# One ring of five PSUM banks for scores and products of maxima, and the product of maxima last in its slot

## The chip, the core and the metric

The kernel runs on one core of a Trainium2 chip. The metric is the device time of one execution in microseconds. Before the change the median of three runs is 2717.88 us (2717.04 to 2718.28). One execution was profiled: 2720.0 us, with 2718.2 us from the first to the last instruction.

Engines are named as in the profile: PE is TensorE's matmuls, PEld its loads of the stationary operand, DVE is VectorE, ACT is ScalarE, POOL is GpSimd, SP is the queue that issues DMAs.

## The reference, cut to what matters

One transformer layer on 2048 rows of width 1024, in float32, followed by a norm. It has a retention branch in two directions, an attention branch and a feed-forward block. What the change touches is the attention:

```python
def _dense_attention(q, k, v):
    s = jnp.einsum('bqkgd,bskd->bkgqs', q, k).astype(jnp.float32) * ATT_SCALE
    p = jax.nn.softmax(s, axis=-1).astype(v.dtype)
    return jnp.einsum('bkgqs,bskd->bqkgd', p, v)
```

There are 8 query heads of width 64 on 2 key heads, and 2304 keys (2048 of the sequence and 256 of the context). A softmax needs the largest score of each row, or a number near it, to be subtracted ahead of the exponential.

## The kernel before, in words

Work on attention is cut into 32 groups: one tile of 128 query rows by one of the two key heads, with its 4 query heads side by side (512 columns). A group goes through two passes over the 2304 keys, 18 steps each.

- First pass, for the row maxima. Step i is `piece` (L164): a product of queries and keys, rows on the partitions and 512 keys across, into a PSUM bank (one matmul, L169, or two half ones, L173). `maximum` (L175) reduces it on DVE to one negated maximum a row (L182). After 18 steps `least` (L184) joins them, `turn` (L190) transposes the result into a PSUM bank with four matmuls (L193), and `rows` (ACT, L196) and `rows2` (DVE, L200) write it as a high and a low part into rows of the query tile `qr`, so that the score matmul adds it.
- Second pass. `scores` (L202) makes the scores turned, 128 keys on the partitions and 512 query columns across: a first matmul (L206) and a second (L207) that holds the subtracted maxima and so needs `qr` from `rows2`. `exp` (L209, ACT) reads the bank, `cast` (ACT, L216) makes a float16 high part of two steps at once, `low` the low part (on POOL, L224, or DVE, L226), and `values` (L228) multiplies both by the values, 24 small matmuls (L240 to L242) for two steps. `combine` (DVE, L247, L252) divides by the sum.

The order on every engine is written out by hand. Time is counted in slots. `on(k, phase, fn)` puts a step into slot k, and a loop over the slots runs the phases of each slot in the order of PHASES. So within each engine the instructions stand in the order slot, phase, and within a phase in the order in which they were registered. An engine never passes a waiting instruction of its own. With 18 slots to a group (NK) and LAG = 22, group n has its piece i in slot 18n + i, the maximum of it one slot later, `least` in slot 18n + 18, `turn` and `rows` in slot 18n + 20, `rows2` in slot 18n + 21, score i in slot 18n + 22 + i, its exponential one slot later, and values j in slot 18n + 22 + 2j + 8, which is always an even slot. So in most slots PE has the score of one group and the piece of the next, and in every second slot values.

Group 0 has its pieces in the stage before, and the last 22 slots have no pieces.

Beside attention the slots carry other work ("pe" is its phase on PE), with a period of 35 slots per tile of rows:

- retention (from slot 66 + 35n): one score step (8 matmuls, L1370), two slots of state products (L1349), four slots of `head` (L1379 to L1381); `mask` and `update` on DVE.
- the output projection, `output_tile`, with k = 109 + 35n: the transposes of retention and attention results at k - 11 and k - 6 (L1475) with `part` behind them (ACT L1480, DVE L1482); output products (three matmuls each, L1490 to L1492) at k plus the 16 PLACES 0 to 3, 5 to 8, 11 to 14 and 16 to 19, the first eight for one half of the columns and the rest for the other half in the same bank, with `add` (DVE, L1497) behind each half in the phase "early" of slots k + 10 and k + 20; then `square` (ACT, L1502) in the phase "cast" of slot k + 20, `norm` (ACT, L1516) in the phase "late" of slots k + 24 and k + 25, its transposes `turn_x` (L1521) in slots k + 25 and k + 27, and `modulate` (DVE, L1526) in the phase "early" one slot behind each.

PSUM has eight banks. In this stage two hold the side work (`bank(0)`, `bank(1)`), one the output of `values`, and five belong to the pool psS: three under the tag "mp", which pieces and the turned tile take in turn, and two under the tag "st", which scores take in turn. A tile that takes a bank waits for the last reader of the tile that had it: a score waits for the exponential of the score two slots earlier, a piece for the maximum of the piece three places earlier.

Of the kernel before, what the change touches and what calls it, by code (L numbers as in the profile page):

```python
# [11 lines left out]
F32 = mybir.dt.float32  # L12
# [10 lines left out]
P = 128  # L23
# [32 lines left out]
def layer_kernel(ctx: ExitStack, tc: tile.TileContext, a: dict, out: bass.AP):  # L56
# [87 lines left out]
    class Group:  # L144
# [43 lines left out]
                nc.vector.tensor_reduce(mt[:, :, c], nm, axis=AX.X, op=ALU.min)  # L188

        def turn(self):  # L190
            self.m = psS.tile([P, 4, P], F32, name="mp", tag="mp", bufs=3)
            for h in range(4):
                nc.tensor.transpose(self.m[:, h], self.mt[:, h], ident)  # L193

# [5 lines left out]
            nc.vector.scalar_tensor_tensor(lo, self.m[96:], 1 / ROW, lo, op0=ALU.mult, op1=ALU.subtract)  # L200

        def scores(self, kt):  # L202
            ps = self.s[kt] = psS.tile([P, 512], F32, name="st", tag="st")
            k = slice(kt * P, (kt + 1) * P)
            q = self.qr.rearrange("p x h t -> p x (h t)")
            mm(ps, ks[:, self.g, k], q[:, 0], start=True, stop=False)  # L206
            mm(ps, ks2[:, self.g, k], q[:, 1], start=False, stop=True)  # L207
# [50 lines left out]
    with ExitStack() as st:  # L258
# [154 lines left out]
        def turned(fn):  # L413
            def turn(x):
                x["ps"] = columns(x["b"][:64], 4)

            def use(x, q):
                at(q, "turn", turn, x)
                at(q + 1, "work", lambda: fn(x["ps"][:, :, :, 0]))

            return use
# [337 lines left out]
        def value_parts(q0):  # L759
# [39 lines left out]
            for i in range(3):  # L799
                at(q0 + 3 + i, "extra", greatest, i)  # L800
                at(q0 + 11 + i, "extra", parts, i)
            at(q0 + 7, "turn", turn)
            at(q0 + 8, "work", scale)

# [25 lines left out]
        def ff_scales(q0):  # L830
# [71 lines left out]
            at(q0, "dma", load)  # L902
            at(q0 + 1, "extra", greatest)
            at(q0 + 3, "turn", turn)
            at(q0 + 4, "work", whole)
            at(q0 + 6, "extra", scales)
# [306 lines left out]
    def pool(stack, name, bufs=1, **kw):  # L1213
        return stack.enter_context(tc.tile_pool(name=name, bufs=bufs, reuse_waits="tile", **kw))
# [4 lines left out]
    psS = pool(attn, "psS", 2, space=PSUM)  # L1219
# [29 lines left out]
    def on(k, phase, fn, *args):  # L1249
        events.setdefault((k, phase), []).append((fn, args))  # L1250

    def run(k, phase):
        for fn, args in events.pop((k, phase), ()):
            fn(*args)


    chain, settled = [], set()
# [21 lines left out]
    def attention():  # L1279
        for n, g in enumerate(groups):  # L1280
            k = NK * n
            if n > 0:
                on(k - 14 if n >= EARLY else k + NK - 6, "dma", g.load)
            else:
                on(k + 2, "dma", g.load)
            if n >= EARLY:
                on(k - 1, "late", g.minima, sm)
                for i in range(NK):
                    on(k + i, "piece", g.piece, i, psS, "mp", 3)
                    on(k + i + 1, "maximum", g.maximum, i)  # L1290
            on(k + NK, "chain", g.least, mts[n % 2])
            on(k + NK + 2, "scores", g.turn)
            on(k + NK + 2, "cast", g.rows)
            on(k + NK + 3, "early", g.rows2)
            k += LAG
            for i in range(NK):
                on(k + i, "scores", g.scores, i)
                on(k + i + 1, "exp", g.exp, i)
            for j in range(NK // 2):
                on(k + 2 * j + 3, "cast", g.cast, j)  # L1300
                if j in POOL_PAIRS:
                    on(k + 2 * j + 4, "low", g.low, j)
                else:
                    for i in range(2):
                        on(k + 2 * j + 4 + i, "low", g.low, j, i)
                on(k + 2 * j + 8, "values", g.values, j)
            k += NK + 7
            on(k, "early", g.combine, ats)
        return NK * len(groups) + LAG + 10
# [301 lines left out]
    for i in range(3):  # L1611
        on(19 + 2 * i, "begin", more_keys, 0, i)
        on(26 + 4 * i, "late", more_keys, 1, i)
    done = attention()
    retention(25)
    output_weights(44)
# [333 lines left out]
    def prelude(k0):  # L1950


        on(k0 - 8, "dma", fetch_w1, 0)
        on(k0 - 2, "late", sum_w1, 0, *SUMS1[0])
        on(k0 - 1, "late", sum_w1, 0, *SUMS1[1])
        on(k0, "begin", open_early)
        for n in range(7):
            on(k0 + (n // 2 if n < 4 else 12 + 2 * n), "dma", fetch_h, 0, n)
            on(k0 + 2 + 2 * n, "late", form_w1, 0, n)
            on(k0 + 3 + 2 * n, "late", lower_w1, 0, n)  # L1960
        on(k0, "late", sum_w1, 0, *SUMS1[2])
        on(k0 + 3, "late", sum_w1, 0, *SUMS1[3])
        on(k0 + 16, "dma", fetch_w1, 1)
        on(k0 - 12, "dma", fetch_gate)
        for i in range(4):
            for k in range(4):
                on(k0 + 14 + 4 * i + k, "pe", up_part, 0, i, k)
            on(k0 + 17 + 4 * i, "late", up_out, 0, i)
            on(k0 + 24 + 2 * i, "late", sum_w1, 1, *SUMS1[i])
# [10 lines left out]
        early_job(b, pairs0 + 60 + 80 * b)  # L1980
    on(made_at + 1, "begin", open_late)
    prelude(done)
    PHASES = ("begin", "scores", "piece", "maximum", "early", "exp", "cast", "low", "chain", "pe", "values")
    PHASES += ("late", "dma")
    with tc.manual_schedule():
        for k in range(min(events)[0], max(events)[0] + 1):
            for phase in PHASES:
                run(k, phase)
# [5 lines left out]
        for b in range(2 * NB):  # L1994
            g = 7 * b
# [51 lines left out]
        g = NU * NS  # L2047
# [15 lines left out]
        for lo, g0 in ((0, g + 10), (4, g + 14)):  # L2063
# [3 lines left out]
            for m in range(lo, lo + 4):  # L2067
                k = g0 + 1 + m % 4 // 2
# [3 lines left out]
        g = NU * (2 * NS - 1)  # L2072
# [125 lines left out]
```

## Time and profile before

| what | value |
|---|---|
| median of three runs | 2717.88 us (2717.04 to 2718.28) |
| the profiled execution | 2720.0 us, span 2718.2 us |
| granted TensorE clock, mean | 0.991 |
| PE busy over the span | 2627.0 us (97%) |
| DVE, ACT, POOL busy over the span | 2101.8, 1585.8, 1416.2 us |
| first and last start of a score matmul (L206) | 626.5 and 1496.5 us |
| PE's wait at L206 for ACT's exponential | 13.5 us in 22 waits |

How to read it: a line of the timeline is start, duration, engine, line, operation, output and inputs, count, and in brackets the idle time of the engine before it with what ended that. The ends of matmuls are modelled, and they overlap: a matmul of 512 columns has 0.38 us in the rows, and the next one can start 0.21 or 0.22 us after it. Idle time counts from the modelled end, and short gaps aren't shown. A row of the table of waits is the waiting instruction, what released it, the total in us, the number of waits and the longest.

### The profile page before, as it was taken

The page shows a single profiled execution, that of the slowest core. Times are in us where ns is not written, and L with a number is a line of the kernel's source. Part 1 is how long each engine was busy: PE and PEld are TensorE (multiplying, and loading weights), DVE is VectorE, ACT ScalarE, POOL GpSimd, SP SyncE. Part 2 cuts the span into 40 slices and gives each one's busy share as a digit, 9 for nine tenths or more (in the row PEclk, how much of TensorE's full clock was granted, in tenths as well). Part 3 has the DMA queues.
Part 4 walks back from the last instruction along what each step waited for, and adds up shares of the span by engine and source line. Part 5 has one row for each costly group of instructions (what it writes and reads, how often), then busy time and mean ns, then how long its engine had stood idle before and what let it go on. Part 6 is the DMA issues. An engine that isn't in the chain of part 4 may idle for free.

```text
span 2718.2 us, 49296 instructions
## 1 busy us (share of the span) xinstructions
PE 2627.0 (97%) x19015; PEld 1418.7 (52%) x19015; DVE 2101.8 (77%) x3323; ACT 1585.8 (58%) x2656; POOL 1416.2 (52%) x1262
## 2 busy tenths in 40 slices
PE   6999999998999999999999899999999999999997
PEld 2545754555666666666666444444444444444443
DVE  4857578878977888888887477898899856666676
ACT  3733763327877778887778475555554554344332
POOL 2623673475656667787777444455557621111155
PEclk8999999999999999999999999999999999999999
DMA  7478858674112223333322655565657332222223
GB/s 253 148 235 293 246 170 274 199 264 150 57 51 68 72 74 93 130 90 122 100 77 80 223 190 175 193 205 188 193 178 269 115 117 86 78 86 86 78 85 132
DMA packets 274197, 402.31 MB, mean 148 GB/s; under 512 B 107237, under 2 KB 162405, under 8 KB 271658
## 3 DMA queue, kind: packets, MB, share of 16 engines
q1 hardware_dynamic: 270938, 394.44, 44.6%
q10 hardware_dynamic: 3024, 4.72, 0.5%
q8 instruction: 149, 2.44, 0.4%
q14 instruction: 86, 0.70, 0.1%
HBM read 294.08 MB, written 105.00 MB: 147 GB/s over the span
## 4 chain that ended last, share of the span: by engine, by line
PE 48%; DVE 4%; ACT 2%; issue 1%; DMA 1%; POOL 0%; SPq 0%; POOLq 0%; ACTq 0%; DVEq 0%
PE pu L1698 7%; PE pu L1700 7%; PE pu L1699 7%; PE pd L1877 6%; PE pd L1875 6%; PE pd L1876 6%; PE st L206 1%; PE st L207 1%; PE mp L169 1%; PE bank L1492 1%; PE bank L1490 1%; PE bank L1491 1%; PE o L240 1%; PE o L242 1%; PE o L241 1%
## 5 line engine op out<-in xcount | busy, mean ns | idle before, releaser
L224 POOL TENSOR_TENSOR plo<-p,phi 128x512 f16<-128x512 f32 x320 | 393.4, 1250 | 165.7 <-ACT phi L216 118.0
L182 DVE TENSOR_REDUCE nm<-mp 128x1 f32<-128x512 f32 (+1 forms) x576 | 386.4, 684 | 118.3 <-PE mp L169 91.6
L212 ACT ACTIVATE p<-st 128x512 f32<-128x512 f32 x576 | 339.6, 600 | 136.5 <-PE st L207 126.5
L1698 PE MATMUL pu<-hf,w1f 128*128 128x512 f16 x896 | 340.6, 380 | 4.8 <-ACT w L1715 4.8
L1700 PE MATMUL pu<-hf,w1f 128*128 128x512 f16 x896 | 340.6, 380 | 0.0
L1699 PE MATMUL pu<-hf,w1f 128*128 128x512 f16 x896 | 340.5, 380 | 0.0
L216 ACT ACTIVATE phi<-p 128x1024 f16<-128x1024 f32 x288 | 304.6, 1058 | 0.0
L642 PE MATMUL pso<-wlo,h 128*128 128x512 f16 (+1 forms) x816 | 295.7, 362 | 2.2 <-DVE wlo L539 2.2
L641 PE MATMUL pso<-whi,h 128*128 128x512 f16 (+1 forms) x816 | 296.0, 363 | 1.3 <-ACT whi L538 1.3
L643 PE MATMUL pso<-whi,h 128*128 128x512 f16 (+1 forms) x816 | 295.7, 362 | 0.0
L226 DVE TENSOR_TENSOR plo<-p,phi 128x512 f16<-128x512 f32 x256 | 231.5, 905 | 12.8 <-ACT phi L216 9.0
L240 PE MATMUL o<-wv,plo 128*128 128x65 f16 x2304 | 237.9, 194 | 1.6 <-DVE ma L252 1.3
L241 PE MATMUL o<-wv,phi 128*128 128x64 f16 x2304 | 237.8, 192 | 0.0
L242 PE MATMUL o<-wv,phi 128*128 128x65 f16 x2304 | 236.8, 193 | 0.0
L206 PE MATMUL st<-qr,ks 128*128 128x512 f16 x576 | 218.7, 380 | 14.1 <-ACT p L212 13.5
L240 PEld LDWEIGHTS <-plo 128*128 128x128 f16 x2304 | 211.3, 97 | 29.3 <-issue 4.7
L1901 DVE SCALAR_TENSOR_TENSOR acc<-pd,scv,acc 128x512 f32<-128x512 f32 x248 | 183.2, 743 | 53.0 <-PE pd L1877 50.3
L241 PEld LDWEIGHTS <-phi 128*128 128x128 f16 x2304 | 210.2, 98 | 25.3
L207 PE MATMUL st<-qr,ks 128*128 128x512 f16 x576 | 217.9, 378 | 3.8 <-DVE qr L200 3.2
L1663 POOL TENSOR_TENSOR w1s<-w1r 128x512 f32<-128x512 f32 x64 | 92.0, 1437 | 231.7 <-ACT w L1737 160.3
L242 PEld LDWEIGHTS <-phi 128*128 128x128 f16 x2304 | 210.5, 97 | 0.0
L169 PE MATMUL mp<-ks,qr 128*128 128x512 f16 x512 | 194.3, 380 | 8.4 <-DMA qr<-aq 5.7
(382 smaller groups left out, 6377.6 us busy)
## 6 DMA issues: line engine op xcount, KB each, us to landing
w2t<-w2f SPq DMA_DIRECT2D x98, 512.0 KB, 4.3
wm<-in_w_ff SPq DMA_DIRECT2D x64, 512.0 KB, 5.5
w1r<-in_w_ff SPq DMA_DIRECT2D x64, 512.0 KB, 4.6
w2f<-w2f SPq DMA_DIRECT2D x98, 256.0 KB, 2.4
wmr<-in_w_mod SPq DMA_DIRECT2D x32, 512.0 KB, 5.0
w2r<-in_w_ff SPq DMA_DIRECT2D x32, 512.0 KB, 4.7
hf<-hp SPq DMA_DIRECT2D x56, 256.0 KB, 3.1
hf<-hf SPq DMA_DIRECT2D x14, 1024.0 KB, 7.2
```

Source lines behind the costliest of these rows:

```text
L182: nc.vector.tensor_reduce(dst, src, axis=AX.X, op=ALU.max, negate=True)
L212: nc.scalar.activation(self.p[kt // 2][:, kt % 2], self.s.pop(kt), AF.Exp, scale=HD**-0.5)
L216: nc.scalar.activation(hi, self.p[j], AF.Copy)
L224: nc.gpsimd.tensor_tensor(lo[:, i], p[:, i], hi[:, i], op=ALU.subtract)
L240: mm(o, lo[:, i, c], v[:, : HD + 1], start=first, stop=False, **more)
L241: mm(o[:, :HD], hi[:, i, c], v[:, VL : VL + HD], start=False, stop=False, **more)
L242: mm(o, hi[:, i, c], v[:, : HD + 1], start=False, stop=last, **more)
L641: mm(self.ps[:, c], hi[:, k], wh, start=k == 0, stop=False)
L642: mm(self.ps[:, c], hi[:, k], wl, start=False, stop=False)
L1698: mm(pu[c], whi, hi, start=first and k == 0, stop=False, **more)
L1699: mm(pu[c], whi, lo, start=False, stop=False, **more)
L1700: mm(pu[c], wlo, hi, start=False, stop=k == 3, **more)
```

## The change

Pieces, the turned tile and scores share one tag, "sp", with five banks, in place of three and two. And the phase "piece" stands behind "values", at the end of PE's work of a slot, in place of right behind "scores". What is computed doesn't change.

```diff
         def turn(self):
-            self.m = psS.tile([P, 4, P], F32, name="mp", tag="mp", bufs=3)
+            self.m = psS.tile([P, 4, P], F32, name="mp", tag="sp", bufs=5)
...
         def scores(self, kt):
-            ps = self.s[kt] = psS.tile([P, 512], F32, name="st", tag="st")
+            ps = self.s[kt] = psS.tile([P, 512], F32, name="st", tag="sp", bufs=5)
...
                 for i in range(NK):
-                    on(k + i, "piece", g.piece, i, psS, "mp", 3)
+                    on(k + i, "piece", g.piece, i, psS, "sp", 5)
                     on(k + i + 1, "maximum", g.maximum, i)
...
-    PHASES = ("begin", "scores", "piece", "maximum", "early", "exp", "cast", "low", "chain", "pe", "values")
+    PHASES = ("begin", "scores", "maximum", "early", "exp", "cast", "low", "chain", "pe", "values", "piece")
     PHASES += ("late", "dma")
```

In PE's order a slot is now score, turned tile where there is one, side work, values, piece. With one score and one piece a slot, the tile five places back is, for a score, the piece of three slots earlier, and for a piece, the score of two slots earlier; so a score waits for DVE's maximum and a piece for ACT's exponential. For two slots behind each turned tile the places are shifted by one.

## The prediction

> **What bounds the kernel now.** I read the page first, then the time by stage, the table of waits of the attention stage, and the timelines of three places in it.
>
> ```profile
> PE 2627.0 (97%) x19015; PEld 1418.7 (52%) x19015; DVE 2101.8 (77%) x3323; ACT 1585.8 (58%) x2656; POOL 1416.2 (52%) x1262
> ```
>
> ```profile
> 626.00:700.00 74.00, 68.57 (x883) 45.43 (x882) 70.95 (x122) 65.54 (x100) 48.52 (x41) 0.99 0.40 130
> 1200.00:1300.00 100.00, 94.35 (x1138) 63.40 (x1137) 88.55 (x150) 78.84 (x122) 78.65 (x68) 1.00 0.37 119
> 626.00:1440.00 814.00, 787.28 (x9545) 523.86 (x9544) 692.10 (x1204) 652.82 (x1014) 575.00 (x509) 1.00 0.29 88
> ```
>
> The columns are the stretch, its length, then PE, PEld, DVE, ACT and POOL busy. The stage that holds both tiles is TensorE's: 787.28 us busy of 814, at the full granted clock (1.00). So at most 27 us of visible gaps are there to be won. VectorE follows at 692.10, with 70.95 of 74 in the opening.
>
> ```profile
> L206 PE MATMUL st<-qr,ks x576: 376/379/631, 626.5 to 1496.5; 128*128 128x512 f16 x192
> ```
>
> ```profile
> DVE nm L182 <- PE mp L169: 87.2, 120, 3.1
> PE st L206 <- ACT p L212: 13.5, 22, 1.5
> ACT junk L1502 <- DVE xr L1497: 9.1, 9, 2.1
> PE st L207 <- DVE qr L200: 3.2, 6, 0.9
> PE mp L169 <- DVE nm L182: 2.6, 2, 2.3
> PE o L240 <- DVE ma L252: 1.3, 2, 0.9
> ```
>
> (us in total, times, longest.) 576 slots start between 626.5 and 1496.5: 1.51 us a slot. The one large wait of TensorE is the one the ring is about: a score bank whose exponential isn't done, 13.5 us in 22 waits. VectorE, on the other hand, waits 87.2 us for the products: its maximum mostly starts when the product is ready, so it follows wherever the product goes.
>
> **The change, part by part.** No instruction is added or removed, no DMA is moved; only TensorE's order and the owners of five banks change. The product is passed by the slot's side products ("pe") and by its values; VectorE's and ScalarE's own orders stay.
>
> *What the ring takes away.* A score now waits for the maximum of three slots ago, and a product for the exponential of two slots ago, about a slot's content later than the score did. The two waits of one tile period:
>
> ```profile
> 768.15 0.38 PE L206 MATMUL st<-qr,ks 128*128 128x512 f16 x1
> 768.36 0.38 PE L207 MATMUL st<-qr,ks 128*128 128x512 f16 x1
> 770.25 0.38 PE L206 MATMUL st<-qr,ks 128*128 128x512 f16 x1 [0.57 <-ACT p L212]
> 774.22 0.66 PE L1521 MATMUL bank<-ident,xn 128*128 128x128 f32 x4
> ```
>
> ```profile
> 768.57 1.06 ACT L1502 ACTIVATE junk<-xr 128x1024 bf16<-128x1024 f32 x1 [0.30 <-DVE xr L1497]
> 769.63 1.06 ACT L212 ACTIVATE p<-st 128x512 f32<-128x512 f32 x2
> 773.43 0.73 ACT L1516 ACTIVATE xn<-xr,cy_f 128x512 f32<-128x512 f32 x1
> ```
>
> A matmul lasts 0.38 but the next starts 0.21 later (768.15, 768.36), so a wait costs its idle plus 0.17: 0.74 at 770.25, and 13.5 + 22 x 0.17 = 17 us for all 22. What is late next: ScalarE has no gap behind the square of 768.57, and the transposes at 774.22 start 0.06 behind the xn that it makes in that same run (773.43 + 0.73). If the score stops waiting at 770.25, TensorE waits that much longer at 774.22. Gain: 0. In every other tile (35 slots a tile, values in every second slot) there is room:
>
> ```profile
> 824.51 0.38 PE L206 MATMUL st<-qr,ks 128*128 128x512 f16 x1 [0.89 <-ACT p L212]
> 829.04 0.60 PE L1521 MATMUL bank<-ident,xn 128*128 128x128 f32 x4
> 831.48 0.38 PE L206 MATMUL st<-qr,ks 128*128 128x512 f16 x1 [0.47 <-ACT p L212]
> ```
>
> ```profile
> 827.68 0.74 ACT L1516 ACTIVATE xn<-xr,cy_f 128x512 f32<-128x512 f32 x1
> ```
>
> Here xn ends at 828.42, 0.62 ahead of 829.04: of the 1.06 at 824.51 some 0.57 is won, and behind the transposes the 0.64 at 831.48 too, 1.2 in all. Some 7 tiles of each kind lie in the stage: 7 x 1.2 = 8 us, and I allow 2 more for the waits of the opening and the end. Against it, the square waits for VectorE's sum (9 of its starts); that sum stands behind a maximum, so it comes about 0.6 later by what follows: 9 x 0.6 = 5 us lost where ScalarE sets the pace. What is left is about 5 us; the bounds are -1 and 17.
>
> *What the later product costs: the row maxima.* VectorE does the maximum first in each slot; what stands behind it comes later too. First the rows2 step (L200), which the next group's second score matmul needs:
>
> ```profile
> 765.91 0.38 PE L169 MATMUL mp<-ks,qr 128*128 128x512 f16 x1
> 766.13 0.38 PE L1490 MATMUL bank<-wo,ah 128*128 128x512 f16 x1
> 766.56 0.38 PE L1492 MATMUL bank<-wo,al 128*128 128x512 f16 x1
> 767.50 0.38 PE L206 MATMUL st<-qr,ks 128*128 128x512 f16 x1
> 767.93 0.38 PE L169 MATMUL mp<-ks,qr 128*128 128x512 f16 x1
> ```
>
> ```profile
> 766.33 0.69 DVE L182 TENSOR_REDUCE nm<-mp 128x1 f32<-128x512 f32 x1 [1.04 <-PE mp L169]
> 767.05 0.70 DVE L200 SCALAR_TENSOR_TENSOR qr<-mp,qr 32x512 f16<-32x512 f32 x1
> 767.78 0.75 DVE L1497 SCALAR_TENSOR_TENSOR xr<-bank,sco,xr 128x512 f32<-128x512 f32 x1
> ```
>
> Now: product 765.91, maximum 0.42 later, rows2 0.72 after that, ended 767.75; the matmul that needs it starts 768.36, 0.6 to spare. After: the product goes behind three matmuls and 24 values, to 767.50 - 0.21 = 767.29; maximum 767.71, rows2 768.43 to 769.13. The matmul stays due at 768.36, so TensorE waits 0.8. Between the two lies just one slot: 0.65 where it holds nothing else (767.50 to 768.15), 0.65 more with three output matmuls, which leaves 0.15. By the planner's places 10 of a tile's 35 slots are empty so: of 30 groups 9 x 0.8 + 21 x 0.1 = 9 us. In 6 of them the matmul waits today (3.2 us), VectorE being late; they pay little more: 8 us. Bounds: 3, where VectorE is late in most groups and the product doesn't set it, and 30 x 0.8 = 24.
>
> *The first half's sum (L1497).* The second half's first output product needs its bank:
>
> ```profile
> 1077.25 0.38 PE L169 MATMUL mp<-ks,qr 128*128 128x512 f16 x1
> 1078.19 0.38 PE L206 MATMUL st<-qr,ks 128*128 128x512 f16 x1
> 1079.27 0.38 PE L169 MATMUL mp<-ks,qr 128*128 128x512 f16 x1
> 1079.48 0.38 PE L1490 MATMUL bank<-wo,rh 128*128 128x512 f16 x1
> ```
>
> ```profile
> 1077.67 0.69 DVE L182 TENSOR_REDUCE nm<-mp 128x1 f32<-128x512 f32 x1 [0.60 <-PE mp L169]
> 1078.39 0.75 DVE L1497 SCALAR_TENSOR_TENSOR xr<-bank,sco,xr 128x512 f32<-128x512 f32 x1
> ```
>
> The product of 1077.25 goes to 1077.98, its maximum to 1078.40, the sum to 1079.12, done 1079.87. The output product, now ahead of its slot's own product, is due at 1079.27: 0.65 of waiting. That holds where the slot between has no values, half of 16 tiles: 5 us (bounds 0 and 10).
>
> *Hand-overs of the same form without a row of their own wait:* the retention scores behind the first modulate (L1526), the attention transposes behind the second, the next group's first values behind combine (L252). Each is one or two VectorE steps behind a maximum and due a slot later. From below 0, from above 0.65 as in the last case: 8 tiles x 2 + 31 x 10/35 groups, 25 x 0.65 = 16. I take half, 8, since a part of these slots is shared with ScalarE's stretch.
>
> *The ring's own new wait.* From a product's end to the score that takes its bank lie two slots (3.0 us) where three lay before the next product. VectorE lags in the opening and at 1200 to 1300 (rows above), and has cost 2.6 us in two waits. From -2.6 (the wait just goes) to 12 (one slot, 1.5, in each of eight such stretches): I take 3, near the row there is.
>
> **Sum:** -5 + 8 + 5 + 8 + 3 = +19. The four losses aren't independent: each holds TensorE while VectorE catches up, and one within ScalarE's stretch costs nothing. I count 15 of the 24: +10 us. The profiled execution took 2720.0, so 2730; the median of the runs lies 2.1 under it, so 2728.
>
> **Rivals.** *Faster:* the ring is worth its whole wait, 17 us with 4 given to VectorE: 2705. For it: 13.5 us is the largest wait, and VectorE is idle for 122 of 814 us, so it could catch up. Against it: the rows at 774.22, and two VectorE steps of 0.7 that don't fit in a slot of 0.65. The Trainium skill speaks for it (Perfetto Trace Analysis, Optimization Strategy): the same gap again and again on the engine that should be full can mean too few buffers. The trace agrees on the wait at 824.51, not on the one at 770.25, where ScalarE is full.
> *No change:* ScalarE's waits go (8 to 10 us) and VectorE, where it is late anyway, costs as much: 2718.
> *Slower by far:* every new wait at its price (24), no gain from ScalarE, and the square late in all tiles: 2742. It decides if the sum of L1497 stands behind a waiting maximum in most tiles.
> *The ring doesn't do what it says:* the turned tile takes a place too, so for two slots after it a score waits for the exponential two back, as before. Price: 2 of 18 slots, under 17 x 2/18 = 2 us of the gain; it changes no sign and is in the cases above.
>
> **How the numbers follow.** Forecast 0.50, with 2723 to 2736 as its own range; slower by far 0.14; no change 0.20; faster 0.16. A measurement of this kernel tells about 0.2% (5.4 us) from no change. So slower 0.64, same 0.20, faster 0.16. The range leaves out the faster half of the faster case and the end of the slowest: 2708 to 2742.
>
> **What would show it.** Right: the score's wait for ScalarE falls from 13.5 to under 5; the second score matmul's for qr grows from 3.2 us in 6 to some 10 in 15 or more; the output product's for the sum appears with about 0.5 a time; x transposes wait for xn; the square waits longer than 9.1. Wrong: if the wait for qr stays under 5 us, the costs of the later product are misjudged, and the time is below 2718.

## The result and the profile after

The changed kernel takes 2758.7 us (median of four runs, 2754.45 to 2761.04) against 2718.08 us (median of four as well): a ratio of 1.0143, with a 95% interval of 1.0131 to 1.0155, some 39 us slower. The profiled execution has a span of 2757.0 us, 38.8 us more than before. The score matmuls now run for 908.0 us, where they ran for 870.0:

```profile
L206 PE MATMUL st<-qr,ks x576: 376/379/634, 623.6 to 1531.6; 128*128 128x512 f16 x192
```

So nearly the whole loss, 38.0 of 38.8 us, lies in the attention stage. The stretch from 626 us to the last score by engine, of the kernel before and then of the changed one (length, then busy time of PE, PEld, DVE, ACT, POOL):

```profile
626.00:1496.50 870.50, 841.54 (x10241) 561.16 (x10240) 729.23 (x1271) 699.91 (x1089) 618.16 (x549) 1.00 0.29 88
```

```profile
626.00:1531.60 905.60, 853.35 (x10239) 559.07 (x10238) 745.70 (x1267) 700.10 (x1086) 622.63 (x548) 0.99 0.27 84
```

TensorE's idle time grows from 29.0 to 52.3 us, by 23.3. Its busy time grows as well, by 11.8 us for the same matmuls. Most of that is waiting too: the modelled matmul lasts 0.17 us longer than its place in the pipeline, so the first 0.17 us of each wait count as busy, and waits shorter than that show no gap at all. Counted from the start of one matmul to the start of the next, what goes beyond the usual distance sums to some 43 us before and to 74 to 79 after, by which distance is taken as usual. So 31 to 36 us of waiting stand against the 35 us by which the stretch is longer.

Rows of the table of waits of this stage in the changed kernel, taken from 596 us on, as before the change (waiting instruction, releaser, us in total, times, longest):

```profile
DVE nm L182 <- PE mp L169: 116.1, 157, 2.9
ACT junk L1502 <- DVE xr L1497: 20.9, 14, 2.1
PEld bank L1521 <- ACT xn L1516: 12.3, 13, 1.8
PE st L207 <- DVE qr L200: 10.1, 20, 0.8
PE bank L1521 <- ACT xn L1516: 6.0, 6, 1.3
PE st L206 <- DVE nm L182: 6.0, 9, 1.6
PE bank L1490 <- DVE xr L1497: 5.8, 9, 1.6
PE bank L1475 <- DVE u L1526: 5.8, 9, 2.0
PE o L240 <- DVE ma L252: 5.4, 7, 1.3
PE st L206 <- ACT p L212: 2.3, 3, 1.0
```

The wait that the ring is about has all but gone (13.5 us before, 2.3 now). In its place stand six TensorE waits of 5 to 10 us: four for a VectorE step that stands behind a maximum (qr, xr, u, ma), one for the maximum itself, which now frees the score's bank, and one for ScalarE's xn. VectorE itself waits longer for the product: 116.1 us, 87.2 before. The place whose rows the prediction works out, in the changed kernel, in order of time:

```profile
768.80 0.38 PE L206 MATMUL st<-qr,ks 128*128 128x512 f16 x1
769.00 0.69 DVE L182 TENSOR_REDUCE nm<-mp 128x1 f32<-128x512 f32 x1 [1.36 <-PE mp L169]
769.72 0.70 DVE L200 SCALAR_TENSOR_TENSOR qr<-mp,qr 32x512 f16<-32x512 f32 x1
770.45 0.75 DVE L1497 SCALAR_TENSOR_TENSOR xr<-bank,sco,xr 128x512 f32<-128x512 f32 x1
770.47 0.38 PE L207 MATMUL st<-qr,ks 128*128 128x512 f16 x1 [0.65 <-DVE qr L200]
771.24 1.06 ACT L1502 ACTIVATE junk<-xr 128x1024 bf16<-128x1024 f32 x1 [1.67 <-DVE xr L1497]
776.10 0.73 ACT L1516 ACTIVATE xn<-xr,cy_f 128x512 f32<-128x512 f32 x1
776.88 0.66 PE L1521 MATMUL bank<-ident,xn 128*128 128x128 f32 x4 [1.27 <-ACT xn L1516]
```

The second score matmul waits 0.65 + 0.17 = 0.82 us for qr; the working gave 0.8. The sum of 770.45 is the step that was priced too low. It ends at 771.20, and the square had been waiting for it for 1.67 us (0.30 before). Counted from the score matmul of its slot (767.50 before, 768.80 here), the square starts 1.37 us later than before, at 2.44 in place of 1.07. ScalarE's run of work starts that much later, and at its end the x transposes wait 1.27 us for xn.

### The profile page after: what moved, and what is told of

Its sections match the earlier page's. It is cut to its first block, busy times and chain, and to the rows that moved or that the text cites. A ratio compares the mean times of both kernels' runs of the same rounds, so it can differ in the third digit from the quotient of the medians.

```text
span 2757.0 us, 49314 instructions
## 1 busy us (share of the span) xinstructions
PE 2639.8 (96%) x19015; PEld 1416.6 (51%) x19015; DVE 2126.2 (77%) x3323; ACT 1588.9 (58%) x2656; POOL 1420.8 (52%) x1262
## 3 DMA queue, kind: packets, MB, share of 16 engines
q8 instruction: 149, 2.44, 0.4%
## 4 chain that ended last, share of the span: by engine, by line
PE 48%; DVE 5%; ACT 2%; issue 1%; DMA 1%; POOL 0%; SPq 0%; POOLq 0%; ACTq 0%; DVEq 0%
PE pu L1698 7%; PE pu L1700 6%; PE pu L1699 6%; PE pd L1877 6%; PE pd L1875 6%; PE pd L1876 6%; PE st L207 1%; PE st L206 1%; DVE nm L182 1%; PE mp L169 1%; PE bank L1490 1%; PE bank L1492 1%; PE bank L1491 1%; PE o L240 1%; DVE w1f L1679 1%
## 5 line engine op out<-in xcount | busy, mean ns | idle before, releaser
L224 POOL TENSOR_TENSOR plo<-p,phi 128x512 f16<-128x512 f32 x320 | 404.0, 1284 | 173.1 <-ACT phi L216 88.8
L226 DVE TENSOR_TENSOR plo<-p,phi 128x512 f16<-128x512 f32 x256 | 248.1, 970 | 16.6 <-ACT phi L216 12.7
L207 PE MATMUL st<-qr,ks 128*128 128x512 f16 x576 | 219.2, 381 | 10.1 <-DVE qr L200 10.1
```

Source lines behind the costliest of these rows:

```text
L224: nc.gpsimd.tensor_tensor(lo[:, i], p[:, i], hi[:, i], op=ALU.subtract)
```

## The experiments

Two theories are told apart. The first: TensorE waits because VectorE's steps stand behind a maximum, and the maximum waits for a product that comes late. The second: the ring itself costs, because a score now needs VectorE's maximum to free its bank. Ratios are to the kernel before, which ran again beside each set of experiments, with 95% intervals.

**The ring alone.** The changed kernel with the product back in its old place:

```diff
-    PHASES = ("begin", "scores", "maximum", "early", "exp", "cast", "low", "chain", "pe", "values", "piece")
+    PHASES = ("begin", "scores", "piece", "maximum", "early", "exp", "cast", "low", "chain", "pe", "values")
```

> The five banks as one ring, the product still right behind the score. Theory (VectorE's steps that feed TensorE stand behind a maximum that waits for a late product): the product isn't late, so the loss is gone; 2705 to 2722 us, the score's wait for ScalarE falls from 13.5 us to under 5, the x transposes' wait for xn grows to 3 to 6 us, the second score matmul's wait for qr stays near 3 us. Rival (the ring itself costs: a score now needs VectorE's maximum to give its bank back): most of the loss stays, 2740 us or more, with waits of the score for the maximum of 10 us or more.

Measured: 1.0001 (0.9991 to 1.0010). No loss, and no gain either. Its waits in the stage:

```profile
PEld bank L1521 <- ACT xn L1516: 8.1, 10, 1.7
PE st L207 <- DVE qr L200: 3.9, 8, 1.1
PE bank L1521 <- ACT xn L1516: 3.4, 7, 0.9
PE mp L169 <- DVE nm L182: 3.0, 4, 2.3
PE o L240 <- DVE ma L252: 3.0, 4, 1.3
PE st L206 <- DVE nm L182: 2.2, 5, 0.6
PE st L206 <- ACT p L212: 0.8, 1, 0.8
```

The score's 13.5 us for ScalarE are 0.8. The x transposes' wait for xn, 0.4 us in two waits before (first row below), has 3.4, and the weight loads ahead of them wait 8.1 (3.8 before, second row). Part of the wait has moved there, as the timeline of before said it would. All gaps of TensorE in the stage together are 23.4 us in 40 waits, against 27.4 in 42 before, in one profiled execution each, and over the runs no time is won that can be told. The new waits for VectorE's maximum are 2.2 + 3.0 us, against 2.6 before. The two rows of the kernel before:

```profile
PE bank L1521 <- ACT xn L1516: 0.4, 2, 0.3
PEld bank L1521 <- ACT xn L1516: 3.8, 7, 0.8
```

**The product last, alone.** The kernel before with the changed line PHASES; three banks and two, as they were.

> The product last in its slot, with three banks for products and two for scores as before the change. Theory: the whole loss is here, and the score's wait for ScalarE stays beside it; 2755 to 2775 us, wait for qr about 10 us in 20. Rival (the ring costs): 2715 to 2730 us.

Measured: 1.0153 (1.0138 to 1.0168), as slow as the change with its ring.

```profile
PE st L206 <- ACT p L212: 22.6, 25, 1.6
PE st L207 <- DVE qr L200: 9.6, 18, 0.9
PE bank L1490 <- DVE xr L1497: 5.6, 9, 1.4
PE bank L1475 <- DVE u L1526: 5.2, 7, 2.0
```

The loss comes with the product's new place, without a ring, and the second theory falls. The score's wait for ScalarE even grows to 22.6 us here, and still the ring, which takes it away, is worth no time that can be told (1.0143 against 1.0153).

**VectorE's early steps ahead of the maximum.** The changed kernel, with two phases exchanged:

```diff
-    PHASES = ("begin", "scores", "maximum", "early", "exp", "cast", "low", "chain", "pe", "values", "piece")
+    PHASES = ("begin", "scores", "early", "maximum", "exp", "cast", "low", "chain", "pe", "values", "piece")
```

> The changed kernel with the phase early (rows2, the sums of L1497, low parts L1482, modulate L1526, combine L252) ahead of the phase maximum, so that in each slot VectorE does them before the maximum that waits. Theory: the waits of TensorE for qr, for the sum, for ma and for u go back to the few us of before, the square waits under 10 us, 2705 to 2725 us. Rival (the ring costs, or the late product does by itself): 2745 us or more.

Measured: 0.9982 (0.9972 to 0.9992). All of the loss is gone, with the product as late as in the change, and the kernel is some 5 us faster than before. The waits for qr, the sum, u and ma in the stage:

```profile
DVE nm L182 <- PE mp L169: 73.4, 115, 2.9
ACT junk L1502 <- DVE xr L1497: 7.6, 8, 1.5
PE bank L1521 <- ACT xn L1516: 3.5, 6, 0.7
PE bank L1475 <- DVE u L1526: 1.4, 2, 1.1
PE o L240 <- DVE ma L252: 1.3, 1, 1.3
PE bank L1490 <- DVE xr L1497: 1.2, 2, 1.0
PE st L207 <- DVE qr L200: 0.8, 1, 0.8
```

The late product costs nothing by itself, and the runs without the ring further down say the same (0.9996 with the product last, 0.9990 with it behind the score). What costs is the order of VectorE's queue: steps that are due in a slot, behind one that waits.

**The product ahead of the values.**

```diff
-    PHASES = ("begin", "scores", "maximum", "early", "exp", "cast", "low", "chain", "pe", "values", "piece")
+    PHASES = ("begin", "scores", "maximum", "early", "exp", "cast", "low", "chain", "pe", "piece", "values")
```

> The changed kernel with the product behind the side work but ahead of the values: it comes late only in slots with side work. Theory: the loss follows how late the product is, and the values (0.73 us in every second slot) make most of it; 2715 to 2738 us. Rival (the ring costs): 2745 us or more.

Measured: 1.0054 (1.0037 to 1.0071), 15 us slower than before. The loss goes with how late the product is: passing the side work costs 15 us, the values some 24 more.

**One step at a time.** The changed kernel with one of the steps of early put into the phase "begin", ahead of the maximum: rows2, the two sums of L1497, combine, or the low parts and modulate.

```diff
-            on(k + NK + 3, "early", g.rows2)
+            on(k + NK + 3, "begin", g.rows2)
```

The others are the same edit on the lines of `add`, of `g.combine`, and of `part(..., 1)` with `modulate`.

> The changed kernel with rows2 alone ahead of the maximum in its slot. Theory A (the hand-overs cost independently, each its whole wait): the waits for qr go, 9 us of gaps, and the second half's sum right behind it comes earlier in some tiles; 2745 to 2751 us. Theory B (the losses overlap by a third or more, as the forecast discounted them): 2752 to 2757 us, other waits growing in the place of this one.

> The changed kernel with the two sums of L1497 alone ahead of the maximum. Theory A: the output product's wait (6.7 us) goes, and the square and with it xn come earlier in 15 tiles, so the x transposes' 6 us shrink as well; 2743 to 2751 us. Theory B: 2752 to 2757 us.

> The changed kernel with combine alone ahead of the maximum. Theory A: the wait of the values for ma (5.4 us) goes; 2751 to 2755 us. Theory B: 2755 to 2758 us.

> The changed kernel with the low parts of L1482 and modulate of L1526 alone ahead of the maximum. Theory A: the waits of the attention transposes and of the retention scores (5.8 us shown, some 9 by the gaps) go; 2747 to 2753 us. Theory B: 2753 to 2757 us.

| moved ahead | ratio | interval | won against 1.0143 |
|---|---|---|---|
| rows2 | 1.0103 | 1.0086 to 1.0120 | 0.0040: 11 us |
| both sums | 1.0071 | 1.0056 to 1.0086 | 0.0072: 20 us |
| combine | 1.0124 | 1.0109 to 1.0139 | 0.0019: 5 us |
| low parts and modulate | 1.0092 | 1.0077 to 1.0107 | 0.0051: 14 us |
| all of them | 0.9982 | 0.9972 to 0.9992 | 0.0161: 44 us |

The us are the difference of the ratios times 2718; by the intervals each is good to 4 to 6 us, so combine's 5 is at the edge of the noise. The four make 50 us against 44 for all at once; the 50 is good to some 15 only, since 1.0143 enters it four times. An overlap of a third would have left some 30. The medians, 2746.3, 2738.0, 2752.5 and 2743.4 us, all lie under the ranges of theory B, which falls. Rows2 and combine lie in the ranges of theory A; the two sums, and the low parts with modulate, won more than either theory expected. The trace of the two sums, in the stage:

```profile
ACT junk L1502 <- DVE xr L1497: 6.5, 7, 1.5
PEld bank L1521 <- ACT xn L1516: 5.4, 10, 1.0
PE st L206 <- DVE nm L182: 3.7, 5, 1.6
PE bank L1490 <- DVE xr L1497: 1.0, 1, 1.0
PE bank L1521 <- ACT xn L1516: 0.6, 1, 0.6
```

The output product's wait went (5.8 to 1.0 us), the square's fell (20.9 to 6.5), and with it the x transposes' wait for xn (6.0 to 0.6); the scores' wait for the maximum fell as well (6.0 to 3.7).

**What ring and place are worth once early is ahead of the maximum.** The same exchange of phases in three more kernels, and in the last the maximum goes behind the phase "low" too.

> The kernel before with the phase early ahead of the maximum, nothing else. If that order helps by itself, without ring and without the late product: 2708 to 2716 us, the waits for qr, ma and the sum (6 us together) gone. If it is only an undoing of the late product: 2716 to 2722 us.

> The ring, the product right behind the score, and the phase early ahead of the maximum. If the ring's gain only moves to the x transposes' wait for xn, as in the ring alone: as the kernel before with early first, within 3 us. If the ring pays once the hand-overs are early: 2704 to 2711 us.

> The product last and early ahead of the maximum, with three and two banks as before the change. Against the changed kernel with early first (2713.8 us) it shows what the ring is worth with a late product: 2725 to 2735 us if the score's wait for ScalarE (22.6 us with the late product alone) comes back as a loss; 2712 to 2717 if the wait only moves.

> Ring, product last, and the phase maximum behind early and low too (the low parts on VectorE no longer stand behind the maximum either). If only the steps of early were due soon, the low parts have slots to spare and nothing more is won; then it is as early first, 2711 to 2717 us, and the scores' wait for the maximum, which now gives the bank back later, grows above 4 us. If the low parts were late as well: under 2708 us. If the ring's wait decides: over 2722 us.

| banks | product | VectorE's order | ratio | interval |
|---|---|---|---|---|
| 3 and 2 | behind the score | early first | 0.9990 | 0.9981 to 0.9999 |
| ring | behind the score | early first | 0.9987 | 0.9978 to 0.9996 |
| 3 and 2 | last | early first | 0.9996 | 0.9987 to 1.0005 |
| ring | last | early first | 0.9982 | 0.9972 to 0.9992 |
| ring | last | early and low first | 0.9992 | 0.9983 to 1.0001 |

The five lie within 0.14% and their intervals overlap. The exchange by itself, in the kernel before, wins 0.0010, some 3 us, and its 2716.5 us lie at the border of the two ranges given for it. The ring with the product behind the score is within 3 us of that (2715.2), as expected of a wait that only moves. The late product without the ring, at 2717.8 us, lies just above the 2712 to 2717 of a wait that only moves and far below the 2725 of a loss. With the product behind the score the ring's 0.0003 is nothing; with it last, 0.0014 may be something, and these runs don't settle it. Moving the maximum behind the low parts too wins nothing: the low parts have slots to spare. The scores' wait for the maximum is then 4.8 us, as that expectation had it. The lowest of the five, the change with early first, beats both kernels, the one before by 0.18% (0.08 to 0.28), but it can't be told from the other four.

## Why the prediction was wrong

Slower was right, and so was the mechanism (VectorE's steps behind a maximum that waits for a late product); the size was not: +10 us forecast, +39 to +41 measured, outside the range of 2708 to 2742. Three steps failed: the delay of the second half's sum, the halving of the hand-overs, and the discount for overlap. Step by step:

- *ScalarE's wait only moves.* Right in kind. The ring alone took the wait away and won nothing (interval -0.09% to +0.10%). Of the 10 us that the forecast still gave it in the other tiles and at the ends, no run shows any that is clear of the noise; that gain with the ring's own new wait of 3 against it would have made the ring alone 7 us faster.
- *rows2.* 8 us forecast, 11 measured by moving it alone. The wait for qr came as worked out: 10.1 us in 20 waits, 0.82 us at the place shown.
- *The first half's sum* was priced at 5, and the second half's, through the square, at another 5. Both together measure 20. The price of the first holds: its wait in the table is 5.8 us in 9, or 7 with 0.17 for each. (The rows of the prediction give 1079.87 - 1079.27 = 0.60 a time where it wrote 0.65; the 5 stays.) The second was mis-sized. A delay of 0.6 in 9 tiles was taken, about what three output products take (0.65), though the prediction's own working at the place shown moves the maximum ahead of that sum by 1.38 (766.33 to 767.71), because there the product passes 24 values too. The square is later by just that, 1.37, at this place. Counted in the same way in both traces, it starts 1.0 to 1.4 us later in seven of the stage's 14 tiles and 0 to 0.6 in the other seven, 11 us in all; in the table it waits 20.9 us in 14 where it had waited 9.1 in 9. With the 7 of the first half that comes near the 20 measured.
- *The hand-overs without a row* were taken at half of their upper bound, 8 of 16. Moving combine, and the low parts with modulate, wins 5 + 14 = 19. The full price was near; the halving had no row behind it.
- *The ring's new wait.* 3 us forecast; the table has 6.0 in the change and 2.2 with the ring alone. Of the right order.
- *The discount.* "I count 15 of the 24" failed. The losses were said to relieve each other, because TensorE's wait lets VectorE catch up. One by one their removal wins 50, together 44, which the intervals don't tell apart, so no relief of that size is seen; why there is so little stays open. Without the discount the forecast would have been 2737, inside the range and still too low. What was missing beyond that is the second half's sum and the other half of the hand-overs.

The rival "slower by far", 2742, was the nearest, with the right reason ("the sum of L1497 stands behind a waiting maximum in most tiles"), and was given 0.14. Its sum, 2718 + 24, has no term for the square, which it names. The rule of the Trainium skill on repeated gaps (Perfetto Trace Analysis, Optimization Strategy), which the prediction set beside the faster case, is that such a gap can mean too few buffers. Here more banks took the gap away (13.5 us to 0.8 in the ring alone) and no time was won, as the row at 774.22 had it. Every sign listed for "right" came: the score's wait for ScalarE under 5, qr at 10 in more than 15, the sum's wait at 0.64 a time, xn, and the square.

## What to carry to other kernels

When a producer is moved later, its consumer's engine is what to look at: the steps behind the waiting consumer in that engine's order move later with it, as rows2 and the sum did behind the maximum of 769.00, and each that is due within about a slot becomes a wait of the bound engine. Here the cure was the order of the consumer's own queue, not more buffers: what is due first goes ahead of what waits. The delay has to be worked out anew for each slot, from what the producer passes there: with side products alone it was about 0.6 us, with the values too about 1.4. The waits added up nearly in full here, so take no discount for overlap, and no half price, without a row that shows it. And follow a late step through the next engine (sum, square, xn, transposes) before calling it small.

## What the runs showed of the hardware

VectorE's busy time in the stage rose by 16.5 us (729.23 to 745.70) with no instruction added. Nearly all of it is in one group, the low parts of L226; the groups of the whole span in the kernel before, in the changed one and in the change with early first:

```profile
L226 DVE TENSOR_TENSOR plo<-p,phi 128x512 f16<-128x512 f32 x256 | 231.5, 905 | 12.8 <-ACT phi L216 9.0 <-POOL plo L224 3.4
```

```profile
L226 DVE TENSOR_TENSOR plo<-p,phi 128x512 f16<-128x512 f32 x256 | 248.1, 970 | 16.6 <-ACT phi L216 12.7 <-POOL plo L224 3.4
```

```profile
L226 DVE TENSOR_TENSOR plo<-p,phi 128x512 f16<-128x512 f32 x256 | 246.1, 962 | 13.1 <-ACT phi L216 9.2 <-POOL plo L224 3.4
```

The mean of one went from 905 to 970 ns, while the maximum's stayed at 684. GpSimd does the other low parts (L224). By the spans of the profile, the low parts beside which GpSimd runs nothing take 0.67 to 0.69 us (72 of the 256 before, 68 in the changed kernel); the others have a mean of 0.99 us before and 1.07 after, and the longest takes 1.84. The Trainium skill (SBUF — State Buffer, Who interferes with whom) says that a VectorE instruction with two inputs in SBUF contends with a GpSimd instruction that reads SBUF, for a port pair that is locked for one of them. The traces agree in that the long ones all stand beside work of GpSimd; no run took that work away, so the cause is argued. It isn't the loss: early first has a mean of 962 ns and is the lowest of all.
